# Projections by Strassen's algorithm ahead of the scan, in a Mamba-2 and gated-MLP encoder layer

## The chip, the cores and the metric

One core of a Trainium2 chip runs one encoder layer for two request groups, 1024 prompt tokens and 64 sample tokens, 1088 in all. The measure is the device time of one execution in microseconds (us); lower is better. The core's engines run side by side, each with its own queue in which instructions are taken in order: TensorE (PE in the profile; its loading of weights is listed as PEld), VectorE (DVE), ScalarE (ACT), GpSimd (POOL) and SyncE (SP, which here only starts DMA transfers).

## The reference, cut to what matters

```python
h = rms_norm(x, pre_mix_w)                        # (1088, 1024)
proj = h @ w_in                                   # (1024, 9248): u 1024, v 1024, z 2048, xBC 3072, dt 32, g_a 1024, g_b 1024
u = gelu(u); v = layer_norm(gelu(v))
o_a = u * (blocked 128x128 position mix of v + bias)
xs, B, C = split(silu(causal_conv(xBC, width=4)))
y = ssd_scan(xs, dt, B, C)                        # 4 groups of 8 heads, row tiles of 128 tokens, state carried from tile to tile
o_b = group_rms_norm((y + d_skip * xs) * silu(z))
merged = sigmoid(g_a) * (o_a @ w_branch_a) + sigmoid(g_b) * (o_b @ w_branch_b)
x = x + rms_norm(merged @ w_out)
x = x + rms_norm(relu(rms_norm(x) @ w_up)**2 @ w_down)
```

## The kernel before, in words

Every big product is made three times over. Each operand is held as a rounded part (`hi`, stored as fp32r) and a remainder (`lo`); `split` writes `hi` on ScalarE (line 80) and `lo` on VectorE or GpSimd (line 81), and the product is hi·hi + hi·lo + lo·hi, accumulated in one PSUM bank. There are two forms. `proj_M` (lines 132 to 134) holds 128 tokens still and moves 512 weight columns, 24 matmuls for a row tile and 512 columns. `proj_T` (lines 118 to 120) holds 128 weight columns still and moves 384 or 320 tokens (`TT`), 24 matmuls for each of three token blocks. 1088 tokens are 9 row tiles (`NT`).

The stages follow one another in the program:

1. `first` norms a row tile of the input, `first_T` transposes it into `hT`, and `z_tile` makes z row tile by row tile with `proj_M` (4 x 9 tiles), storing silu pieces in `z_d`; `dt_part` runs among them. The first product needs one row tile only. `v_part` does the same for v (2 x 9 tiles) with gelu and layer norm (STT at line 226, bias at line 227).
2. For each of the 4 groups, `xbc_chunk` makes six 128-column chunks of xBC with `proj_T`, the convolution as one ScalarE pass and three VectorE passes (line 430) for each token block, and transposes to token order. Then the group's scan runs over its 9 row tiles, software-pipelined: `stage_a` (decay matrices: GpSimd line 511, ScalarE line 514, VectorE line 515, and three GpSimd products, lines 519 to 522), one `next(gates)`, which is 24 `proj_T` matmuls of a gate block, then `stage_b` (matmuls `yd`, `yo`, `sn`; VectorE lines 546 to 558, one GpSimd add at line 551) and `stage_c` (four transposes and a store to `ob_d`).
3. `u_chunk` makes u in eight chunks with `proj_T`, and `spatial` mixes positions and multiplies.
4. The branch products: `w_branch_a` on `oa`, then `w_branch_b` in two halves, gate factors applied by `gated` (line 687).
5. `w_out`, then the feed-forward network. Its up product (`UpW`, `up_pass`, lines 966 to 968) and its down product (lines 1116 to 1118) already use the Strassen-Winograd scheme: seven half-size products where eight would be needed, with sums of weight blocks (`UpW.sums`, lines 868 to 875) and of token blocks. The up product moves 272 tokens (`TQ`), the down product moves 512 weight columns.

Tile pools with a fixed number of buffers (`bufs`) set how far a transfer or an engine can run ahead; a scheduler puts each engine's instructions in one fixed order when the kernel is built. Loads go through SP's queue; most stores go through ScalarE's and GpSimd's queues.

## Time and profile before

| | us |
|---|---|
| median of 3 runs | 2266.93 (2264.79 to 2267.3) |
| profiled execution, its own time | 2264.54 |
| span of its trace, first to last instruction | 2262.7 |
| TensorE busy | 2193.6 |
| VectorE busy | 1323.5 |
| ScalarE busy | 924.7 |
| GpSimd busy | 818.9 |

Busy times of different engines overlap. TensorE counts as busy from the start of a matmul to its modelled end, and matmuls overlap in its pipeline, so its pace is read from counts in a stretch, not from the busy share alone.

### The profile page before, as it was taken

To read this page: it belongs to the slowest core of one execution; us is meant where nothing else is said; L and a number is where in the kernel's file an instruction comes from. 1 tells how busy PE (TensorE), PEld (TensorE's weight loads), DVE (VectorE), ACT (ScalarE), POOL (GpSimd) and SP (SyncE) were. 2 spreads that over 40 slices of the span, in tenths; PEclk is the share of its full clock that TensorE was granted. 3 is DMA by queue.
4 is the path that set the end of the run, shared out by engine and by line. 5 is a ranking of instruction groups with operands and counts; after the bars stand their busy time and mean duration, and the time that the engine had idled before them with its cause. 6 is when DMAs were issued, how large, how long until landed. Compare 5 with 4: busy or idle time off the path is not lost.

```text
span 2262.7 us, 33194 instructions
## 1 busy us (share of the span) xinstructions
PE 2193.6 (97%) x12674; PEld 1966.6 (87%) x12674; DVE 1323.5 (58%) x1850; ACT 924.7 (41%) x1788; POOL 818.9 (36%) x798
## 2 busy tenths in 40 slices
PE   8999999999999989999999999998999998999997
PEld 6777778989979979889999999777999997788786
DVE  5322255677677667655722257377555556577777
ACT  5212255445445455433311133255555555433333
...
PEclk9999999999999999999999999999999999999999
...
GB/s 183 70 84 109 58 84 115 58 144 97 80 138 81 105 125 69 129 126 76 97 173 130 134 119 166 135 172 114 147 152 148 140 148 244 163 116 131 172 119 114
DMA packets 315464, 281.07 MB, mean 124 GB/s; under 512 B 40043, under 2 KB 281389, under 8 KB 314793
## 3 DMA queue, kind: packets, MB, share of 16 engines
q1 hardware_dynamic: 283336, 240.71, 35.8%
...
q8 instruction: 100, 1.64, 0.3%
q14 instruction: 60, 0.48, 0.1%
HBM read 203.96 MB, written 74.93 MB: 123 GB/s over the span
## 4 chain that ended last, share of the span: by engine, by line
PE 67%; issue 12%; POOL 8%; DVE 5%; DMA 4%; ACT 3%; SPq 0%; ACTq 0%; POOLq 0%; DVEq 0%
PE ps L119 8%; PE ps L118 8%; PE ps L120 8%; PE X L968 3%; PE X L966 3%; PE X L967 3%; PE X L1117 3%; PE X L1118 3%; PE X L1116 3%; PE ps L1117 2%; PE ps L1116 2%; PE ps L1118 2%; DMA raw<-w_branch_b 2%; PE ps L706 2%; PE ps L705 2%
## 5 line engine op out<-in xcount | busy, mean ns | idle before, releaser
L118 PE MATMUL ps<-hTh,wh 128*128 128x384 f32 (+1 forms) x1152 | 384.4, 334 | 5.5 <-ACT raw L419 5.5
L120 PE MATMUL ps<-hTh,wl 128*128 128x384 f32 (+1 forms) x1152 | 386.4, 335 | 0.0
L119 PE MATMUL ps<-hTl,wh 128*128 128x384 f32 (+1 forms) x1152 | 384.5, 334 | 0.0
L81 POOL TENSOR_TENSOR wl<-raw,wh 128x1024 fp32r<-128x1024 f32 x74 | 182.4, 2467 | 270.3 <-ACT wh L80 268.0
L80 ACT ACTIVATE wh<-raw 128x1024 fp32r<-128x1024 f32 x128 | 135.3, 1057 | 268.9 <-PE ps L119 98.2
L118 PEld LDWEIGHTS ps<-hTh,wh 128*128 128x128 f32 x1152 | 217.1, 188 | 11.6 <-ACT raw L419 6.0
L120 PEld LDWEIGHTS ps<-hTh,wl 128*128 128x128 f32 x1152 | 216.9, 188 | 9.8 <-issue 9.7
L119 PEld LDWEIGHTS ps<-hTl,wh 128*128 128x128 f32 x1152 | 217.2, 189 | 7.9 <-issue 7.3
L132 PE MATMUL ps<-wh,hTh 128*128 128x512 f32 (+1 forms) x432 | 171.3, 398 | 1.0 <-ACT hTh L177 0.9
L133 PE MATMUL ps<-wl,hTh 128*128 128x512 f32 (+1 forms) x432 | 170.4, 396 | 0.9 <-DVE wl L81 0.9
L134 PE MATMUL ps<-wh,hTl 128*128 128x512 f32 (+1 forms) x432 | 171.0, 396 | 0.2 <-DVE hTl L178 0.2
L430 DVE SCALAR_TENSOR_TENSOR acc<-raw,cw,acc 128x384 f32<-128x384 f32 (+1 forms) x216 | 134.6, 626 | 33.6 <-ACT acc L428 27.7
L966 PE MATMUL X<-hb,wu 128*128 128x272 f32 x512 | 147.7, 291 | 1.9 <-ACT ev L973 1.0
L967 PE MATMUL X<-hb,wu 128*128 128x272 f32 x512 | 147.6, 289 | 0.3 <-DVE hb L790 0.3
L968 PE MATMUL X<-hb,wu 128*128 128x272 f32 x512 | 146.1, 290 | 0.0
L514 ACT ACTIVATE bc<-bc,pcum 128x128 f32<-128x128 f32 (+1 forms) x288 | 90.8, 384 | 89.3 <-POOL bc L511 88.4
L1110 POOL TENSOR_TENSOR wd<-wd,wd 128x1024 f32<-128x1024 f32 x32 | 85.8, 2684 | 113.6 <-DVE dl L81 74.5
L705 PE MATMUL ps<-ob,wh 128*128 128x384 f32 (+1 forms) x384 | 125.4, 327 | 0.0
L706 PE MATMUL ps<-ob,wl 128*128 128x384 f32 (+1 forms) x384 | 125.4, 327 | 0.0
L704 PE MATMUL ps<-ob,wh 128*128 128x384 f32 (+1 forms) x384 | 125.4, 326 | 0.0
L80 ACT ACTIVATE dh<-wd 128x1024 fp32r<-128x1024 f32 x56 | 59.1, 1055 | 153.2 <-PE ps L1117 91.9
L81 DVE TENSOR_TENSOR dl<-xd,dh 128x1024 fp32r<-128x1024 f32 x56 | 100.4, 1818 | 1.8 <-PE X L968 1.2
...
## 6 DMA issues: line engine op xcount, KB each, us to landing
...
xd<-rc_d SPq DMA_DIRECT2D x112, 256.0 KB, 3.9
...
wd<-w_down SPq DMA_DIRECT2D x16, 1024.0 KB, 6.0
...
```

Source lines behind the costliest of these rows:

```text
L80: s.activation(hi, src, AF.Copy)
L81: (lo_eng or v).tensor_tensor(out=lo, in0=src, in1=hi, op=ALU.subtract)
L118: pe.matmul(ps[:, :n], wh[:, k, :], hh[:, k, :n], start=(k == 0), stop=False)
L119: pe.matmul(ps[:, :n], wh[:, k, :], hl[:, k, :n], start=False, stop=False)
L120: pe.matmul(ps[:, :n], wl[:, k, :], hh[:, k, :n], start=False, stop=(k == 7))
L132: pe.matmul(ps[:R, :], hh[:, k, o:o + R], wh[:, kk, :], start=(k == 0), stop=False)
L134: pe.matmul(ps[:R, :], hl[:, k, o:o + R], wh[:, kk, :], start=False, stop=(k == 7))
L705: pe.matmul(ps[:, :n], wh[:, k, :], ob[:, 4 + kk, :], start=False, stop=False)
L706: pe.matmul(ps[:, :n], wl[:, k, :], ob[:, kk, :], start=False, stop=(k == 7))
L966: pe.matmul(ps, wh[:, k, :], bh[:, k, :], start=start and k == 0, stop=False, skip_group_check=chain)
L967: pe.matmul(ps, wh[:, k, :], bl[:, k, :], start=False, stop=False, skip_group_check=chain)
L968: pe.matmul(ps, wl[:, k, :], bh[:, k, :], start=False, stop=k == 3, skip_group_check=chain)
```

## The change

All products of the normed input move into one first stage and use the Strassen-Winograd scheme.

- The normed rows are written once into seven block combinations, each as hi and lo and for two token halves (`hb`, 28 tiles of 4 x 272). Rows 0 to 3 give two of them at once; `second(m)` norms row 4 + m, makes the differences and the other five by transposes (`put`).
- z and v: three passes of 1024 columns (`plan`), each seven products of 4 row blocks x 12 matmuls with 512 moving columns. The weight sums are built by GpSimd from pieces loaded again for each product (`build`). The 64 sample tokens get 8 matmuls in each of four products (`sample`).
- u, xBC and the gates: 24 pairs of chunks (256 columns), each two token halves (`t_pass`) of seven products x 12 matmuls with 272 moving tokens. What used to follow a chunk follows in steps between the products of the next pass (`todo`): gelu and the layer norm of v (`ln_row`) for u, the convolution over 1091 columns at a time for xBC (`x_conv`), tanh for the gates; dt and the spatial mix run among the gate passes (`side`). Results go to DRAM: u, the gates, xs, B and C, the layer-normed v, the dt tables and the branch-A input.
- The scan then runs alone over all 36 (group, row tile) pairs in one pipeline with a load step (`stage_0`) one tile ahead. Between two tiles comes one block of the branch products (`fill`: 24 blocks of branch A, then 24 of the first half of branch B), merged through `mg_d` in DRAM. The add at line 551 moves from GpSimd to VectorE.
- All DMA transfers of these stages go through SP's queue. The second half of branch B, `w_out` and the feed-forward network stay, with other buffers out of the same pools.

```diff
-    ws0 += list(ws)
-    ws = ws0
-    first(2)
-    first_T(1)
-    for i in range(NT):
-        z_tile(ws, 0, i)
...
-    for gi in range(1, G):
...
-        for i in range(NT):
-            z_tile(ws, gi, i)
-            next(dtg, None)
...
-gates = gate_gen()
-for _ in range(3):
-    next(gates)
...
-                next(gates)
...
-                g.tensor_tensor(out=y[:R], in0=y[:R], in1=xi[:R], op=ALU.add)
...
+    def sums(self, k):
+        x, tt = self.src, self.eng.tensor_tensor
+        if k == 0:
+            x["s1"], x["s2"] = (t.rearrange("p (k n) -> p k n", k=4) for t in self.t12)
+            tt(out=x["s1"], in0=x["a21"], in1=x["a22"], op=ALU.add)
+            tt(out=x["s2"], in0=x["s1"], in1=x["a11"], op=ALU.subtract)
+        elif k == 1:
+            x["s3"] = x["a21"]
+            y = (x["a21"], x["a11"]) if self.flip else (x["a11"], x["a21"])
+            tt(out=x["s3"], in0=y[0], in1=y[1], op=ALU.subtract)
+        else:
+            x["s4"] = x["a12"]
+            tt(out=x["s4"], in0=x["a12"], in1=x["s2"], op=ALU.subtract)
...
+def t_pass(w, wn, tt, hbt, evs, ev, xp, todo):
...
+    def prod(j, ps, start=True, chain=True):
+        wh, wl = w.w[j]
+        bh, bl = hbt(TB[j], tt)
+        for k in range(4):
+            pe.matmul(ps, wh[:, k, :], bh[:, k, :], start=start and k == 0, stop=False, skip_group_check=chain)
+            pe.matmul(ps, wh[:, k, :], bl[:, k, :], start=False, stop=False, skip_group_check=chain)
+            pe.matmul(ps, wl[:, k, :], bh[:, k, :], start=False, stop=k == 3, skip_group_check=chain)
...
+    if first:
+        wn.sums(0)
+    step(0)
+    prod(1, Z, chain=False)
+    ev[0](Z, s0)
...
+hb = [[[hbp.tile([P, 4, TQ], F32R, tag="hb", bufs=28, name="hb") for x in "hl"] for tt in range(2)] for n in range(7)]
...
+    def k4(name):
+        return pm.tile([P, 1024], F32, tag="k4", bufs=6, name=name)
...
+    def second(m):
+        row_norm(4 + m)
+        xa, xb = rows[m], rows[4 + m]
+        b12, b22 = xb[:, 0:512], xb[:, 512:1024]
+        e1, e4 = xa[:, 0:512], xa[:, 512:1024]
+        e3 = s2("e3")
+        v.tensor_tensor(out=e1, in0=b12, in1=e1, op=ALU.subtract)
+        v.tensor_tensor(out=e3, in0=b12, in1=b22, op=ALU.subtract)
+        v.tensor_tensor(out=b12, in0=b22, in1=e1, op=ALU.subtract)
+        put(b12, 4, m)
+        put(e3, 5, m)
+        put(e1, 3, m)
+        v.tensor_tensor(out=e4, in0=e4, in1=b12, op=ALU.subtract)
+        put(e4, 6, m)
+        put(b22, 2, m)
...
+    plan = [(pr, n) for pr in range(3) for n in ("P2", "P1", "P6", "P5", "P7", "P3", "P4")]
...
+        elif n == "P6":
+            t = kept[pr, q] = w_piece(pr, 1, 1, q, "v2", True)
+            u = w_piece(pr, 0, 0, q, "w11", False)
+            tt_(out=t, in0=t, in1=u, op=ALU.subtract)
+            u = w_piece(pr, 0, 1, q, "w12", False)
+            tt_(out=t, in0=t, in1=u, op=ALU.add)
...
+    def raw(j):
+        return wpool.tile([P, 1024], F32, tag="raw", bufs=2, name="wr")
...
+    cols = [OFF_U + p * 256 for p in range(4)] + [OFF_X + p * 256 for p in range(12)] + [OFF_GA + p * 256 for p in range(8)]
...
+    def passes(k, ev, after=None, more=None):
+        nonlocal todo
+        for tt in range(2):
+            fs, post = ev(tt)
+            t_pass(W[k], W.get(k + 1), tt, hbt, evs, fs, xp, todo)
+            todo = post
+            if more:
+                more()
+        new_w(k + 2)
...
+    def c_layout(c, dst, p, tt):
+        for h in range(2):
+            d = dst[2 * p:2 * p + 2].rearrange("j p c -> p j c")
+            nc.sync.dma_start(out=d[:, :, h * 512 + tt * 256:h * 512 + tt * 256 + 256], in_=c[:, 2 * h:2 * h + 2, 0:256])
+            nc.sync.dma_start(out=d[:, :, 1024 + h * 32 + tt * 16:1024 + h * 32 + tt * 16 + 16], in_=c[:, 2 * h:2 * h + 2, 256:TQ])
...
+        def ln_row(i):
+            R = ROWS[i]
+            vt = pu.tile([P, D], F32, tag="vt", bufs=2, name="vt")
+            nc.sync.dma_start(out=vt[:R], in_=v_d[i * P:i * P + R, :])
...
+            v.scalar_tensor_tensor(out=vt[:R], in0=vt[:R], scalar=r[:R], in1=lnw[:R], op0=ALU.mult, op1=ALU.mult)
+            g.tensor_tensor(out=vt[:R], in0=vt[:R], in1=lnb[:R], op=ALU.add)
+            nc.sync.dma_start(out=vn_d[i * P:i * P + R, :], in_=vt[:R])
...
+                def p0():
+                    q[0] = pu.tile([P, 4 * TQ], F32, tag="q", bufs=1, name="q")
+                    s.activation(q[0], C, AF.Square)
+                def p1():
+                    g.tensor_scalar(out=q[0], in0=q[0], scalar1=GC * GA3, scalar2=GC, op0=ALU.mult, op1=ALU.add)
+                def p2():
+                    v.tensor_tensor(out=q[0], in0=C, in1=q[0], op=ALU.mult)
+                def p3():
+                    s.activation(q[0], q[0], AF.Tanh)
+                def p4():
+                    v.scalar_tensor_tensor(out=C, in0=q[0], scalar=1.0, in1=C, op0=ALU.add, op1=ALU.mult)
...
+            def tap(k):
+                v.scalar_tensor_tensor(out=t[0][:, :L], in0=r[:, k:k + L], scalar=cw[:, k * 24 + c:k * 24 + c + 1],
+                                       in1=t[0][:, :L], op0=ALU.mult, op1=ALU.add)
...
+            def p5():
+                v.scalar_tensor_tensor(out=t[0][:, :L], in0=r[:, :L], scalar=1.0, in1=t[0][:, :L], op0=ALU.add, op1=ALU.mult)
...
+        def side():
+            with tc.tile_pool(name="pdt", bufs=1, side="right") as wk:
+                yield from dt_part(wk)
+            yield
+            with tc.tile_pool(name="psp", bufs=1, side="right") as wk:
+                for c in range(8):
+                    yield from spatial(c, wk)
...
+    def fill_a(ts):
+        for c in range(8):
+            w = wT(a["w_branch_a"][0], c * P, lo_eng=(v, g)[c % 2])
+            for t in ts:
+                o, n = TT[t]
+                gtt = gate_in(sp, c, t)
+                gated(gtt, proj_T(w, oa, t), gtt[:, :n], n)
+                nc.sync.dma_start(out=mg_d[c][:, o:o + n], in_=gtt[:, :n])
+                yield
...
+    def fill_b(ts):
...
+                gtt = gate_in(sp, 8 + c, t)
+                mgt = sp.tile([P, 384], F32, tag="mgt", bufs=2, name="mgt")
+                nc.sync.dma_start(out=mgt[:, :n], in_=mg_d[c][:, o:o + n])
+                gated(gtt, proj_b(w, 0, t), gtt[:, :n], n)
+                v.tensor_tensor(out=gtt[:, :n], in0=mgt[:, :n], in1=gtt[:, :n], op=ALU.add)
+                nc.sync.dma_start(out=mg_d[c][:, o:o + n], in_=gtt[:, :n])
+                yield
...
+    def fill():
+        for t in range(3):
+            load_oa(t)
+        yield from fill_a((0, 1))
+        for t in range(2):
+            load_ob(0, t, bslot(t, "ob0"))
+        yield from fill_a((2,))
+        for t in range(2):
+            load_ob(1, t, bslot(t, "ob1"))
+        yield from fill_b((0, 1))
+        for gi in range(2):
+            load_ob(gi, 2, bslot(2, f"ob{gi}"))
+        yield from fill_b((2,))
...
+    def stage_0(gi, i):
...
+        d["BT"], d["CT"], d["btok"] = (sp.tile([P, P], F32, tag=n, bufs=3, name=n) for n in ("BT", "CT", "btok"))
+        nc.sync.dma_start(out=d["BT"][:, :R], in_=bc_d[gi][:, tok:tok + R])
+        nc.sync.dma_start(out=d["CT"][:, :R], in_=bc_d[4 + gi][:, tok:tok + R])
...
+            bc = sp.tile([P, 4, P], F32, tag="bc", bufs=6, name="bc")
+            nc.sync.dma_start(out=bc[:R, :, :R], in_=ac_d[h0:h0 + 4, i, 0:R].partition_broadcast(R))
...
+        d["xs"] = sp.tile([P, 512], F32, tag="xs", bufs=3, name="xs")
+        nc.sync.dma_start(out=d["xs"][:R], in_=xs_d[tok:tok + R, gi * 512:(gi + 1) * 512])
+        nc.sync.dma_start(out=d["btok"][:R], in_=btok_d[tok:tok + R, gi * P:(gi + 1) * P])
+        d["sz"] = sp.tile([P, 512], F32, tag="sz", bufs=3, name="sz")
+        nc.sync.dma_start(out=d["sz"][:R], in_=z_d[tok:tok + R, gi * 512:(gi + 1) * 512])
...
+            v.tensor_tensor(out=y[:R], in0=y[:R], in1=xi[:R], op=ALU.add)
...
+    tiles = [(gi, i) for gi in range(G) for i in order]
+    NR = len(tiles)
+    S = None
+    for k in range(NR + 3):
+        if k < NR:
+            stage_0(*tiles[k])
+        if 1 <= k <= NR:
+            stage_a(*tiles[k - 1])
+        if k >= 1:
+            next(filler, None)
+        if 2 <= k <= NR + 1:
+            gi, i = tiles[k - 2]
+            S = stage_b(gi, i, S)
+            if i in (7, 8):
+                state_out(gi, i, S)
+        if k >= 3:
+            stage_c(*tiles[k - 3])
+    for _ in filler:
         pass
```

## Rows read from the trace of the kernel before

**Rows 1.** The page's first part, and its granted-clock line over 40 slices:
```profile
PE 2193.6 (97%) x12674; PEld 1966.6 (87%) x12674; DVE 1323.5 (58%) x1850; ACT 924.7 (41%) x1788; POOL 818.9 (36%) x798
...
PEclk9999999999999999999999999999999999999999
```

**Rows 2.** Busy time by stage (stretch, its length, engines' busy us with counts, clock, DMA):
```profile
0.00:336.60 336.60, 326.30 (x1462) 253.88 (x1463) 126.80 (x163) 107.26 (x160) 68.86 (x109) 1.00 0.31 99
336.60:1002.00 665.40, 640.21 (x3915) 587.02 (x3914) 461.42 (x687) 326.93 (x809) 338.89 (x397) 0.99 0.37 104
1002.00:1137.00 135.00, 135.00 (x855) 133.43 (x855) 80.66 (x155) 45.83 (x87) 38.94 (x36) 1.00 0.32 92
1137.00:1421.50 284.50, 284.50 (x1730) 284.50 (x1729) 115.36 (x123) 66.59 (x72) 119.10 (x62) 1.00 0.48 147
1421.50:2262.70 841.20, 807.61 (x4720) 707.77 (x4719) 539.28 (x724) 378.05 (x661) 253.10 (x195) 0.98 0.47 148
```

**Rows 3.** The same view inside four stretches of one kind of product:
```profile
150.00:250.00 100.00, 100.00 (x432) 78.28 (x431) 23.13 (x27) 20.95 (x29) 10.53 (x18) 1.00 0.30 101
1150.00:1300.00 150.00, 150.00 (x912) 150.00 (x911) 31.98 (x47) 20.99 (x19) 50.57 (x29) 1.00 0.45 139
1600.00:1850.00 250.00, 250.00 (x1989) 250.00 (x1988) 140.42 (x248) 136.40 (x272) 61.67 (x48) 1.00 0.48 147
2000.00:2200.00 200.00, 200.00 (x867) 160.31 (x866) 147.42 (x148) 69.53 (x79) 58.26 (x26) 1.00 0.45 138
```

**Rows 4.** TensorE in order of time at the start (start, length, instruction, count):
```profile
11.16 0.79 PE L132 MATMUL ps<-wh,hTh 128*128 128x512 f32 x1 [0.91 <-ACT hTh L177]
...
15.90 1.03 PE L174 MATMUL tp<-ident,xn 128*128 128x128 f32 x8
```

**Rows 5.** One GpSimd group, each shape apart (busy us, mean ns):
```profile
L227 POOL TENSOR_TENSOR vst<-vst,lnb 128x1024 f32<-128x1024 f32 x8 | 19.3, 2410 | 3.7 <-DVE vst L226 3.7
```

**Rows 6.** VectorE groups of the kind that the passes hold, same view:
```profile
L884 DVE TENSOR_TENSOR wu<-wr,wu 128x512 fp32r<-128x512 f32 x80 | 55.7, 699 | 17.6 <-ACT wu L880 17.5
...
L979 DVE TENSOR_TENSOR C<-Z,ev 128x272 f32<-128x272 f32 x32 | 14.1, 442 | 19.9 <-PE Z L968 15.0 <-ACT C L1034 2.7 <-ACT C L1025 0.7
...
L226 DVE SCALAR_TENSOR_TENSOR vst<-vst,rs,lnw 128x1024 f32<-128x1024 f32 x8 | 10.2, 1279 | 0.7 <-POOL rs L142 0.6
```

**Rows 7.** Busy time in the last scan and two other stretches, as rows 2:
```profile
948.00:1002.00 54.00, 51.10 (x305) 43.91 (x304) 38.79 (x47) 23.39 (x63) 38.50 (x43) 1.00 0.51 141
2050.00:2100.00 50.00, 50.00 (x218) 40.20 (x217) 40.32 (x39) 14.87 (x16) 21.86 (x9) 1.00 0.42 126
1850.00:1900.00 50.00, 50.00 (x389) 49.49 (x388) 25.14 (x46) 25.70 (x49) 4.68 (x3) 1.00 0.76 243
```

**Rows 8.** VectorE groups of the scan, view as rows 5:
```profile
L515 DVE TENSOR_TENSOR bc<-bc,cb 128x512 f32<-128x512 f32 x64 | 42.7, 679 | 14.7 <-POOL xs L522 6.1 <-PE cb L503 4.8 <-ACT bc L514 3.5
...
L558 DVE SCALAR_TENSOR_TENSOR y<-y,rs,snw 128x512 f32<-128x512 f32 x32 | 35.8, 1117 | 20.9 <-POOL rs L142 20.6
...
L546 DVE TENSOR_TENSOR S<-S,elast 128x512 f32<-128x512 f32 x32 | 32.9, 1027 | 0.6
L554 DVE TENSOR_TENSOR y<-y,sz 128x512 f32<-128x512 f32 x32 | 32.4, 1012 | 28.0 <-POOL y L551 27.9
...
L548 DVE TENSOR_TENSOR S<-tp,S 128x512 f32<-128x512 f32 x32 | 21.8, 682 | 1.2 <-PE tp L540 1.2
```

**Rows 9.** VectorE groups that go with the branch products, view as rows 5:
```profile
L81 DVE TENSOR_TENSOR wl<-raw,wh 128x1024 fp32r<-128x1024 f32 x54 | 71.7, 1332 | 43.4 <-ACT wh L80 43.3
...
L687 DVE SCALAR_TENSOR_TENSOR gtt<-gtt,ps 128x384 f32<-128x384 f32 x32 | 17.6, 549 | 42.5 <-PE ps L706 37.8 <-DMA gtt<-gates_d 4.3
...
L81 DVE TENSOR_TENSOR ob<-st,ob 128x1536 fp32r<-128x1536 f32 x8 | 14.0, 1771 | 9.6 <-ACT ob L80 9.5
```

**Rows 10.** One VectorE line of the scan (durations min/median/max):
```profile
L546 DVE TENSOR_TENSOR S<-S,elast x32: 675/1055/1574, 444.1 to 988.7; 128x512 f32<-128x512 f32 x32
```

**Rows 11.** DMA issues (KB each, median us to landing), from 1850 to 1900 us:
```profile
wd<-w_down SPq DMA_DIRECT2D x4, 1024.0 KB, 10.1
```

1247 lines of the change are left out of this document (764 added, 483 removed).

## The prediction

> **What bounds the kernel now.** First the engines' busy shares and the granted clock [rows 1]: TensorE is busy 97% of the span and its granted clock is 0.9 or more of the upper level (2.4 GHz) in every slice, so time is saved by giving TensorE less to stream, as long as no other engine takes over. VectorE is next with 58%, but that is a mean over unlike stages. So the second view is the busy time by stage [rows 2]: the normed input's z and v (0 to 336.6), xBC, scans and most gates (to 1002.0), the last gates and u (to 1137.0), the branch products (to 1421.5), then `w_out` and the feed-forward network (841.2 us). The change touches the first 1421.5 us. VectorE is busy 0.38, 0.69, 0.60 and 0.41 of the four stages, GpSimd 0.51 of the second.
>
> The third view gives TensorE's pace, since busy time cannot [rows 3]: 100 us / 432 = 0.2315 us for a matmul with 512 moving columns, 150 / 912 = 0.1645 with 384 and 320, 250 / 1989 = 0.1257 with 272 (the up product), 200 / 867 = 0.2307 with 512 in the down product. The reader should see that the pace does not fall in proportion: 272 columns are 0.75 of the mean 363, but cost 0.764. That is a small fixed part, and the two Strassen products run at it without a gap.
>
> **z and v.** Before: 54 tiles x 24 = 1296 matmuls x 0.2315 = 300.0, 72 transposes at 1.03 / 8 = 0.129 [rows 4] = 9.3, dt 72 x 0.1645 = 11.8; the remaining 336.6 - 321.1 = 15.5 is the start (the first matmul is at 11.16 [rows 4]) and small waits. After: three passes of 7 x 4 x 12 + 4 x 8 = 368 matmuls, 1104 x 0.2307 = 254.7, and 112 + 8 transposes = 15.5. The start is not shown. From below it is the old 15.5. From above: six buffers hold the norm weight and rows 0 to 3 and 8, so row 5 is loaded only when `second(0)` is through, and the first product P6 waits for the rows; four times a norm (1.28), four differences (1.03 each) and five evictions (0.68 each) (all priced as in the parts below) are 35 us of VectorE against 22 us of P2 and P1, so some 13 more, 29. I take 18, near the lower end, because P5 can go between. Sum 288.2, a gain of 48.4. The weight sums are GpSimd's: ten 1024-wide operations a pass at 2.4 [rows 5] are 24 of 85 us, hidden; without that cover they would be 72.
>
> **u, xBC and gates.** Before, 48 chunks x 72 x 0.1645 = 568.5; after, 24 pairs x 168 x 0.1257 = 506.8, a gain of 61.7. dt moves here: 120 x 0.1257 = 15.1. The transposes to token order and the spatial mix stay: some 220 + 144 instructions at 0.129 = 47. So 569 us of TensorE. What can hold it back is VectorE, in whose queue the evictions that free PSUM stand behind the convolution. A u pass has TensorE at 84 x 0.1257 = 10.56; VectorE has 3.5 splits at 0.70, three evictions at 0.44, two 1088-wide operations at 1.28 x 1088/1024 = 1.36 [rows 6], and 9/8 of a layer-norm row (about 2.56): 9.4. An xBC pass has TensorE at 11.7 with nine transposes; VectorE has four 1091-wide operations (5.5), 2.45 of splits and 1.9 of evictions, 9.8, which is 0.84. Between nothing and the full excess of a slot with eviction, tap and split over one product (some 1 us) I take 0.5 for an xBC pass, 12 in 24, and 0.6 for a u pass, 5 in 8. Gate passes have half of that load: nothing. Three joints between pools: 11. Sum 596.5. The loads for pair k + 2 are asked for after pair k and land within a pass.
>
> **From there to the scan:** tables and first tiles must be loaded and the branch-A input split before TensorE has work: between 5 and 20, taken as 12.
>
> **The scan.** In the last scan before, 305 matmuls ran in 54 us for seven tiles [rows 7]. 7 x 26 are the scan's, the other 123 are gate blocks and cost 123 x 0.1645 = 20.2; (51.1 - 20.2) / 7 = 4.4 us of TensorE for a tile. With a filler block of 24 x 0.1645 = 3.95 a tile needs 8.35. About 40 of the 48 blocks fall into the scan: 36 x 4.4 + 40 x 3.95 = 316 of TensorE. VectorE, from its own rows: two at 0.68, the decay product 1.03, three with a PSUM operand at 0.68, 1.01 and 1.12 [rows 8], and the moved add, priced as the decay product at 1.03 (both operands in SBUF): 7.59. For 36 tiles, less 4 x 2.74 where a group starts with no state, 262. State copies 12 x 0.68 = 8; 40 `gated` at 0.55 = 22; 16 merges at about the same = 9; half of 24 weight splits at 1.33 = 16; ten splits of branch inputs at 1.77 = 18 [rows 9]. Together 335: VectorE, not TensorE, bounds this stage, with 9.3 us a tile where TensorE wants 8.35. From below the stage takes TensorE's 316 (if the contention inside these means goes with GpSimd's add); from above, VectorE reached 40.32 of 50 at most, 0.81, in any stretch I looked at [rows 7], so 335 / 0.81 = 414. I take 0.92, as VectorE was never the bound in those stretches: 364.
>
> **After it:** 8 blocks left, 31.6; the second half of branch B 24 x 3.95 = 94.8; joint 6. Sum 132.4. The rest, 841.2 us [rows 2], changes only in which buffers it takes: nothing, give or take 5.
>
> **The sum:** 288.2 + 596.5 + 12 + 364 + 132.4 = 1393 against 1421.5, so 28.4 less: a span of 2234.3. The profiled execution took 1.8 more than its span, and the median of the runs is 2.4 above that execution: 2238, say 2237, 1.3% faster.
>
> **The rivals.**
> *TensorE keeps the scan (0.15).* If VectorE stays off the path, the scan takes 316, 48 less: 2189. For it: the contended means of [rows 8] (line 546 takes 0.675 to 1.574 [rows 10]) would shrink when GpSimd loses an add. Against: GpSimd gets weight splits in return.
> *VectorE holds the scan at its old share (0.22, the other side).* One mechanism, one place: VectorE's fixed order in the scan, where the chain of one tile (square on ScalarE, root on GpSimd, line 558) leaves holes: 20.6 us of its idle time were waits for that root [rows 8]. At 0.81 the stage takes 414, 50 more than my sum: 2287. It decides from 364 + 28 = 392 us, 10.9 us a tile.
> *VectorE and GpSimd take turns (0.10).* Line 546 has both operands in SBUF and takes 0.675 at best and 1.574 at worst [rows 10], while line 548, with one operand in PSUM, has a mean of 0.682 [rows 8]: such operations wait for GpSimd's. If they exclude each other fully, the u passes are hit: VectorE's two-operand work is 3.5 x 0.70 + 2 x 1.36 + 1.44 = 6.6, GpSimd's two sums (2.4), one 1088-wide operation (up to 2.56) and 9/8 of 2.41 [rows 5] are 7.7; 14.3 against 10.56 is 30 in 8 passes, 25 more than in my sum: 2262, next to no gain. Against: the means that I add up hold these waits already. The Trainium skill (SBUF — State Buffer, section "SBUF: two separate sides") says the same as a rule: a VectorE instruction with two SBUF inputs and a GpSimd one that reads SBUF lock each other out of a shared port pair for a whole instruction. By that rule the u stage would be the loss, and the spread of line 546 agrees with it.
> *Late loads (0.05).* Everything goes through one queue, and the scan moves 36 tiles (51 MB), 24 weight chunks (13), gates and merged blocks (17) and branch inputs (8): 89 MB in 364 us, 244 GB/s. The stretch with 243 GB/s had the DMA engines busy 0.76 [rows 7] and 1 MB loads landing after 10.1 us [rows 11]; `stage_0` asks one tile, about 10 us, ahead. Two us late for each tile would be 72: 2309.
> *The narrow matmuls give nothing back (0.03).* At 568.5 / 4032 = 0.141 a matmul the passes cost what the chunks did: 2299. Against: 1989 at 0.1257 without a gap [rows 3].
>
> **How the numbers follow.** My own case (0.45) is 2237, by its own terms 2215 to 2262. With the two rivals around it, TensorE's scan below and VectorE's above, the range is 2185 to 2290; the late loads and the narrow matmuls stay outside. A measurement of this kernel tells some 0.2% (4.5 us) from no change. Slower takes the three rivals above 2271 less a little (0.27); no change gets part of the turn-taking and the upper end of my case (0.07); faster the rest, 0.66.
>
> **What would show it.** Right: a first `t_pass` near 290 us; up to the scan near 900; passes at 10.6 us for gates and 12.1 for xBC; output stores of the scan about 10 us apart, with VectorE busy over 0.9 there and TensorE some 0.85; the stage behind the branches still 841. Wrong: a scan with VectorE at 0.8 and tiles 11 us apart, or waits of TensorE in the xBC passes for evictions by VectorE, or loads of the scan that land after their tile's turn. My weakest number is VectorE's share in the scan: 0.01 of it is 4 us.

## The result and the profile after

The changed kernel takes 2370.49 us (median of four runs, 2366.20 to 2383.30) against 2265.86 (2264.19 to 2267.30): a ratio of 1.0471 [1.0429, 1.0514], 105 us slower. The forecast was 2237, with a range up to 2290; the time lies outside it on the side that had 0.27. The profiled execution took 2383.3 us, with a span of 2381.5, the longest of the four; a second profile of the same kernel (c0_after) has a span of 2369.2.

The page's first part and its granted-clock line over 40 slices, to be read against [rows 1]:

```profile
PE 2153.5 (90%) x13154; PEld 1926.8 (81%) x13154; DVE 1610.6 (68%) x2086; ACT 1039.9 (44%) x1985; POOL 929.5 (39%) x812
...
PEclk8899999899999999799999989999999999999999
```

TensorE is busy 40 us less than before, as the change meant, but in a span 119 us longer: its share falls from 97 to 90%. VectorE gains 287 us of work. The granted clock falls under 0.9 of the upper level in five slices, which it did in none before. Busy time by stage, as [rows 2], with the boundaries at the first `t_pass` matmul, the last one, the scan's first product, its last store to `ob_d` and the last branch product; then two stretches of the first stage:

```profile
0.00:330.20 330.20, 285.50 (x1225) 225.91 (x1226) 208.51 (x233) 139.47 (x235) 119.10 (x89) 0.95 0.54 164
330.20:983.00 652.80, 587.97 (x4510) 575.22 (x4509) 459.36 (x640) 303.66 (x600) 233.69 (x236) 0.96 0.42 126
983.00:996.00 13.00, 1.36 (x8) 0.84 (x6) 0.00 (x0) 1.35 (x3) 2.34 (x1) 0.61 0.83 222
996.00:1382.70 386.70, 343.46 (x1946) 292.75 (x1946) 319.50 (x404) 170.18 (x432) 252.16 (x264) 0.94 0.85 243
1382.70:1533.30 150.60, 125.69 (x757) 122.80 (x756) 87.09 (x87) 48.14 (x56) 68.08 (x28) 0.93 0.71 215
1533.30:2381.50 848.20, 809.47 (x4717) 709.30 (x4716) 536.14 (x724) 377.10 (x661) 254.09 (x195) 0.98 0.46 147
0.00:100.00 100.00, 57.54 (x245) 43.82 (x246) 64.01 (x75) 42.13 (x92) 44.58 (x49) 0.86 0.43 135
200.00:330.20 130.20, 130.03 (x562) 103.89 (x561) 82.81 (x97) 56.53 (x84) 43.31 (x28) 1.00 0.50 151
```

| stage | forecast | after | too short by | c0_after |
|---|---|---|---|---|
| z and v | 288.2 | 330.2 | 42 | 328.8 |
| passes of u, xBC, gates | 596.5 | 652.8 | 56 | 648.2 |
| to the scan | 12 | 13.0 | 1 | 12.9 |
| scan, first product to last store | 364 | 386.7 | 23 | 382.7 |
| rest of the branches | 132.4 | 150.6 | 18 | 149.3 |
| `w_out` and feed-forward | 841.2 | 848.2 | 7 | 847.3 |

Every term erred to the same side. Three places show how.

**The start.** The first 100 us hold 245 TensorE instructions, 435 before. About 120 are transposes: 120 x 0.129 + 125 x 0.2307 = 44 us of work, 56 lost where I had put 18. The timeline of SP's queue, rows of the input alone (`row_load`, line 321):

```profile
3.43 1.03 SPq L321 DMA_DIRECT2D row<-x_prompt  x2
4.50 0.57 SPq L321 DMA_DIRECT2D row<-x_sample  x1
...
39.41 0.34 SPq L321 DMA_DIRECT2D row<-x_prompt  x1
...
53.10 1.22 SPq L321 DMA_DIRECT2D row<-x_prompt  x2
...
67.58 0.33 SPq L321 DMA_DIRECT2D row<-x_prompt  x1
```

Row 4 is asked for at 39.4, when the sample row has left its buffer, rows 5 and 6 at 53, row 7 at 68: each `second(m)` waits for its row, and P6, the first product that needs these rows, for all four.

**The joint between u and xBC.** The timeline of ScalarE, GpSimd and VectorE, three instructions of the last layer-norm row, the first write to xBC's tile `R`, and the eviction of the first product of three passes (line 239, one in each pass; the expectations below call it the second):

```profile
428.13 0.38 ACT L239 ACTIVATE ev<-X 128x272 f32<-128x272 f32 x1
438.69 0.40 ACT L239 ACTIVATE ev<-X 128x272 f32<-128x272 f32 x1 [0.47 <-DVE C L629]
...
468.19 1.21 DVE L663 TENSOR_REDUCE mu<-vt 64x1 f32<-64x1024 f32 x1 [2.92 <-DMA vt<-v_d]
...
473.01 1.28 DVE L670 SCALAR_TENSOR_TENSOR vt<-vt,rs,lnw 64x1024 f32<-64x1024 f32 x1 [3.61 <-POOL rs L129]
...
474.36 2.33 POOL L671 TENSOR_TENSOR vt<-vt,lnb 64x1024 f32<-64x1024 f32 x1 [1.39 <-DVE vt L670]
...
481.25 0.42 DVE L738 TENSOR_TENSOR R<-Z,ev 128x256 f32<-128x256 f32 x1 [6.96 <-DMA new_gmlp_v_sample<-vt]
...
481.79 0.40 ACT L239 ACTIVATE ev<-X 128x272 f32<-128x272 f32 x1 [9.72 <-DVE R L739]
```

The first xBC pass has its product by 438.7, but may write `R` only at 481.25, when the store of the last layer-norm row has left the memory that `R` takes over. TensorE stands still; the next such step comes 43.1 us on, in place of 12.

**The operations of the passes.** Groups of VectorE and GpSimd in the xBC passes (490 to 755 us), mean ns of one; priced in the forecast at 1360, 700 and 2400 / 2 [rows 5, 6]:

```profile
L772 DVE SCALAR_TENSOR_TENSOR acc<-R,cw,acc 128x1091 f32<-128x1091 f32 x65 | 112.7, 1753 | 13.1 <-ACT acc L769 12.8
L204 DVE TENSOR_TENSOR wu<-wr,wu 128x512 fp32r<-128x512 f32 x53 | 45.3, 862 | 18.4 <-ACT wu L200 17.6 <-PE tp L794 0.6
...
L192 POOL TENSOR_TENSOR wr<-wr 128x512 f32<-128x512 f32 x11 | 23.4, 2128 | 0.0
```

### The profile page after: what moved, and what is told of

The parts are those of the page before. It is cut to its first block, busy times and chain, and to the rows that moved or that the text cites. A ratio compares the mean times of both kernels' runs of the same rounds, so it can differ in the third digit from the quotient of the medians.

```text
span 2381.5 us, 35955 instructions
## 1 busy us (share of the span) xinstructions
PE 2153.5 (90%) x13154; PEld 1926.8 (81%) x13154; DVE 1610.6 (68%) x2086; ACT 1039.9 (44%) x1985; POOL 929.5 (39%) x812
## 4 chain that ended last, share of the span: by engine, by line
PE 42%; DMA 12%; DVE 12%; issue 5%; ACT 4%; POOL 3%; SPq 1%; ACTq 0%; DVEq 0%; POOLq 0%
PE X L1487 3%; PE X L1489 3%; PE X L1488 3%; DVE acc L772 3%; PE X L1638 2%; PE X L1639 2%; PE X L1637 2%; DMA wr<-w_in 2%; PE ps L1638 2%; PE ps L1639 2%; PE ps L1637 2%; DMA xs<-xs_d 2%; DVE wu L204 2%; DMA mg_d<-gtt 1%; PE Y L1487 1%
## 5 line engine op out<-in xcount | busy, mean ns | idle before, releaser
L226 PE MATMUL X<-hb,wu 128*128 128x272 f32 x768 | 228.9, 299 | 26.4 <-ACT ev L252 9.4
L227 PE MATMUL X<-hb,wu 128*128 128x272 f32 x768 | 224.6, 293 | 0.0
L228 PE MATMUL X<-hb,wu 128*128 128x272 f32 x768 | 224.1, 294 | 0.0
L79 POOL TENSOR_TENSOR wl<-raw,wh 128x1024 fp32r<-128x1024 f32 x52 | 129.0, 2485 | 167.5 <-ACT wh L78 121.9
L226 PEld LDWEIGHTS X<-hb,wu 128*128 128x128 f32 x768 | 147.8, 193 | 32.1 <-ACT ev L252 11.5
L1041 PE MATMUL ps<-ob,wh 128*128 128x384 f32 (+1 forms) x384 | 131.2, 343 | 24.4 <-DMA st<-ob_d 18.7
L1487 PE MATMUL X<-hb,wu 128*128 128x272 f32 x512 | 148.3, 291 | 4.1 <-ACT ev L1510 2.3
L227 PEld LDWEIGHTS X<-hb,wu 128*128 128x128 f32 x768 | 148.3, 193 | 0.1
L1488 PE MATMUL X<-hb,wu 128*128 128x272 f32 x512 | 148.0, 290 | 0.0
L1489 PE MATMUL X<-hb,wu 128*128 128x272 f32 x512 | 146.7, 291 | 0.9 <-DVE wu L1405 0.9
L228 PEld LDWEIGHTS X<-hb,wu 128*128 128x128 f32 x768 | 147.4, 193 | 0.0
L204 DVE TENSOR_TENSOR wu<-wr,wu 128x512 fp32r<-128x512 f32 x120 | 103.3, 867 | 51.4 <-ACT wu L200 50.6
L772 DVE SCALAR_TENSOR_TENSOR acc<-R,cw,acc 128x1091 f32<-128x1091 f32 x72 | 124.2, 1742 | 16.0 <-ACT acc L769 15.8
L1631 POOL TENSOR_TENSOR wd<-wd,wd 128x1024 f32<-128x1024 f32 x32 | 85.7, 2681 | 116.5 <-DVE dl L79 77.8
L1042 PE MATMUL ps<-ob,wh 128*128 128x384 f32 (+1 forms) x384 | 129.6, 338 | 0.5 <-DVE ob L79 0.5
L78 ACT ACTIVATE wh<-raw 128x1024 fp32r<-128x1024 f32 x72 | 75.8, 1055 | 103.2 <-DMA raw<-w_branch_b 61.1
L226 PE MATMUL Y<-hb,wu 128*128 128x272 f32 x384 | 113.3, 295 | 7.8 <-ACT wu L200 6.1
L227 PE MATMUL Y<-hb,wu 128*128 128x272 f32 x384 | 112.3, 293 | 0.0
L228 PE MATMUL Y<-hb,wu 128*128 128x272 f32 x384 | 112.0, 293 | 0.0
```

Of the source, the lines that this page charges most:

```text
L78: s.activation(hi, src, AF.Copy)
L204: v.tensor_tensor(out=l, in0=self.src[TN[j]], in1=h, op=ALU.subtract)
L226: pe.matmul(ps, wh[:, k, :], bh[:, k, :], start=start and k == 0, stop=False, skip_group_check=chain)
L227: pe.matmul(ps, wh[:, k, :], bl[:, k, :], start=False, stop=False, skip_group_check=chain)
L228: pe.matmul(ps, wl[:, k, :], bh[:, k, :], start=False, stop=k == 3, skip_group_check=chain)
L772: v.scalar_tensor_tensor(out=t[0][:, :L], in0=r[:, k:k + L], scalar=cw[:, k * 24 + c:k * 24 + c + 1], in1=t[0][:, :L], op0=ALU.mult, op1=A ...
```

## The experiments

The theories, as the expectations number them. **1:** one queue; a store that waits for its producer holds up the loads behind it. **2:** VectorE's own work, with its waits for the root on GpSimd, sets the scan. **3:** late releases of tiles (rows at the start, one pool after another at the joints). **Lock:** VectorE's operations with both operands in SBUF wait while GpSimd's run. **4:** the scan's loads come late. **5:** the traffic of the blocks slows the scan. **6:** no engine alone.

All runs, with the end of the first stage, the length of the passes, and the mean step between the scan's 36 stores to `ob_d`. Kernels that leave a stage alone end the first at 326.5 to 333.9, take 648 to 653 for the passes and 10.4 to 10.7 for a tile; the four totals of the changed kernel span 17 us. What is smaller is not read.

| run | us | z, v end | passes | tile |
|---|---|---|---|---|
| c0_after | 2371.0 | 328.8 | 648.2 | 10.36 |
| e1_store_q | 2382.8 | 325.9 | 661.1 | 10.57 |
| e2_ln_late | 2407.8 | 328.0 | 682.3 | 10.73 |
| e8_row8 | 2365.8 | 321.0 | 650.1 | 10.45 |
| e13_start | 2368.9 | 316.2 | 652.9 | 10.49 |
| e6_nosums | 2333.9 | 327.8 | 606.4 | 10.54 |
| e12_sums_v | 2359.1 | 328.8 | 629.4 | 10.50 |
| e14_ln2 | 2382.6 | 328.3 | 659.3 | 10.47 |
| e7_ob_early | 2351.2 | 328.9 | 650.7 | 10.43 |
| e3_scan_alone | 2385.4 | 330.1 | 649.9 | 9.98 |
| e4_deep | 2368.6 | 328.3 | 650.2 | 10.33 |
| e10_bare | 2257.0 | 329.6 | 653.1 | 8.10 |
| e11_root | 2375.8 | 326.5 | 651.1 | 10.50 |
| e15_relief | 2390.3 | 333.9 | 650.4 | 10.42 |
| e16_norm_act | 2359.4 | 329.6 | 648.5 | 10.09 |
| e17_traffic | 2377.4 | 327.5 | 651.4 | 10.59 |
| c2_all (median of 4) | 2358.2 | 316.9 | 639.9 | 10.51 |
| c4_parts (median of 5) | 2320.7 | 314.9 | 628.1 | 10.36 |

### The kernel again, and the queue

> The changed kernel as it is, for a second profile beside the first one. Every theory expects the same stage times as in the first: products of z and v 330 us, the passes of u, xBC and the gates 653, from there to the start of the second half of branch B 406, then 144, then 848; a few us less in all, since the first profile is of the slowest of four runs (2383 against 2366 to 2373). What differs between the two by more than that is spread, and no experiment is read finer than it.

```diff
...
-nc.sync.dma_start(out=mg_d[c][:, o:o + n], in_=gtt[:, :n])
+nc.scalar.dma_start(out=mg_d[c][:, o:o + n], in_=gtt[:, :n])
...
```

> Every store of the new stages (z, v, u, layer-normed v, xs, B, C, dt tables, gates, branch-A input, merged blocks, scan outputs and states) goes through ScalarE's queue in place of SP's, as most did before the change; loads stay with SP. Theory 1 (one queue: a store that waits for its producer holds up the loads behind it, which is where the late weights and the late loads of the scan come from): TensorE's idle time falls in the u passes, at the joint between u and xBC and in the scan, tiles of the scan go from 10.5 to about 9.3 us, and the whole gains 60 us or more. Theory 2 (VectorE's own chain in the scan, through the root on GpSimd, sets the pace there) and theory 3 (late releases of tiles, at the start and where one pool follows another): within 15 us of the changed kernel, with the hole at the joint and the 56 us lost in the first 100 still there.

It gained nothing: the passes took 13 us more and the tile did not move. The eight u passes (eight steps between evictions of first products) went from 100.7 to 110.6. Theory 1 falls, as far as a store's place in SP's queue goes.

### The start

```diff
-rows[i] = k4("row")
+rows[i] = k4("row") if i < 8 else wpool.tile([P, 1024], F32, tag="raw", bufs=2, name="row")
```

> At the start the sample row (row 8) is put into one of the two buffers for raw weight pieces, so that one of the six row buffers is free and row 4 is loaded at once, not after the sample row has been transposed at 39 us. Theory 3 (buffers: each second(m) waits for a row that could not be loaded yet): the first second() comes about 10 us earlier and the stage of z and v ends at about 315 to 322 in place of 330. Theory 2 applied to the start (VectorE and GpSimd in each other's way, row norms and weight splits): no earlier end, within 4 us of 330.

and in e13_start also

```diff
-split(src[k, q], hi, lo, g if k < 3 else v)
+split(src[k, q], hi, lo, v)
```

> Beside row 8 in a raw buffer (8 us gained in the first stage), the remainders of the first three products' weights are made by VectorE and not by GpSimd, whose 2.5 us each fall together with row norms and differences that took 2.3 to 5.7 us where others of the same shape took 0.7 to 1.3. Lock theory at the start: those fall to 0.7 to 1.3, and the first stage ends 8 to 15 us earlier than with the buffer alone, near 308. Buffers alone: no further gain, within 4 us of 321.

321.0 and 316.2. The buffer gave 8 us, as theory 3 said. The remainders gave 5 more, between what the lock (8 to 15) and buffers alone (less than 4) asked for; that is less than the spread of this stage, but the two later kernels that hold both edits end it at 316.9 and 314.9. TensorE has done 247 instructions by 100 us in c0_after, 280 in e8_row8 and 298 in e13_start. Together the two edits are 13 of the 42 us. In e13_start rows 5 and 6 are still asked for at 41 us and row 7 at 56, so most of the start is still there, in buffers and in the chain of row norms; it wasn't tried further. The totals of these two runs don't show the gain, which is of the size of their spread.

### The layer-norm rows

In e2_ln_late `ln_row` goes from the last step of a u pass into `side()`, ahead of dt:

```diff
 def side():
+    with tc.tile_pool(name="pln", bufs=1, side="right") as pln:
...
+        for i in range(NT):
+            ln_row(i)
+            if i % 3 == 2:
+                yield
```

> The layer norm of v, nine rows, moves from the u passes to the first gate passes, three rows at a time ahead of the dt part. Theory 3 (the first xBC pass writes into memory that the last layer-norm row holds, and waits for its store): the hole of 34 us at the joint goes, u passes fall from 12.6 us to about 11, and the gate passes take some 5 to 8 us more; 35 to 45 us less in all. Theory 1 (the queue alone holds the u passes and the joint): the weights of the next pair stay late, and less than 15 us are gained.

The eight u passes fell from 100.7 to 85.7 us (10.7 a pass; the forecast has 10.56 of TensorE), the step at the joint from 43.2 to 18.9: 39 us gained there, as theory 3 said. But the gate passes took 73 more. Who TensorE waited for in them:

```profile
PE ps L845 <- ACT wdh L78: 58.4, 1, 58.4
```

dt's first product stands in TensorE's queue behind few passes, and its operand is made in a pool that opens when the last row is through. The hole moved with the rows.

```diff
-if lnq:
-    ln_row(lnq.pop(0))
-if len(lnq) == 1:
-    ln_row(lnq.pop(0))
+for _ in range(2):
+    if lnq:
+        ln_row(lnq.pop(0))
```

> The nine layer-norm rows of v go two to a pass into the first u passes, in place of one to a pass with the last two behind the last u pass. Same work on every engine, an earlier place. Theory 3 (the hole at the joint is the chain of the last rows up to their store, which holds the memory that the first xBC pass writes): the step from the last u pass's to the first xBC pass's second eviction falls from 43 us to 20 or less, the u passes take up to 10 us more together, and 10 to 25 us are gained. If the memory of the pool is not what is waited for, the joint stays over 35 us.

The joint fell to 21.2, as expected, but the u passes rose from 100.7 to 133.0: 11 us lost in the passes. So no place that was tried is free of the price. A row is a chain over four queues (load, sum on VectorE, mean on GpSimd, two passes on ScalarE, root on GpSimd, VectorE, GpSimd, store), and what stands behind a link in its queue waits with it; that this chain is the price was read from the waits, not shown by a run that shortens it. Nine rows cost 39 us where they are, and more in both other places.

### The weight sums and the lock

In e6_nosums `TPair.sums` does nothing and the products use plain blocks; in e12_sums_v it runs on VectorE:

```diff
-W[k] = TPair(w_in, cols[k], raw, factor, t12, g if k else v, True)
+W[k] = TPair(w_in, cols[k], raw, factor, t12, v, True)
```

> The passes of u, xBC and the gates leave out GpSimd's four weight sums for each pair of chunks (the products use plain blocks instead of the sums, so u, xBC and the gates are other numbers; everything else is as before). Lock theory (VectorE's operations with both operands in SBUF wait while GpSimd's run): the convolution's tap falls from a mean of 1.74 us towards its shortest, 1.36, the remainders of the weight splits from 0.87 to about 0.70, and a pass of xBC from 11.9 to about 11.2, 20 to 30 us in all. Rival (the means are long because of DMA traffic or the tap's own shape): taps stay at 1.7 us, and the passes gain less than 8 us.

The same groups in the same stretch, without the sums:

```profile
L762 DVE SCALAR_TENSOR_TENSOR acc<-R,cw,acc 128x1091 f32<-128x1091 f32 x67 | 89.9, 1351 | 11.3 <-ACT acc L759 10.9 <-POOL cst L757 0.3
L194 DVE TENSOR_TENSOR wu<-wr,wu 128x512 fp32r<-128x512 f32 x83 | 56.2, 687 | 21.0 <-ACT wu L190 17.4 <-PE tp L784 3.0
```

The tap falls from 1753 to 1351 ns, the remainder from 862 to 687, and the passes by 42 us. Nothing else in the tap changed: it had waited for GpSimd. In the changed kernel the 27 of its 65 taps that have no GpSimd operation beside them take 1347 ns in the mean, the 38 others 2041. One that starts while a sum runs ends 1.16 us after it (timelines of GpSimd and VectorE, the changed kernel):

```profile
502.07 1.76 POOL L195 TENSOR_TENSOR wr<-wr,t 128x512 f32<-128x512 f32 x1
503.01 1.98 DVE L772 SCALAR_TENSOR_TENSOR acc<-R,cw,acc 128x1091 f32<-128x1091 f32 x1
...
506.12 1.34 DVE L772 SCALAR_TENSOR_TENSOR acc<-R,cw,acc 128x1091 f32<-128x1091 f32 x1
```

The Trainium skill (SBUF — State Buffer, section "SBUF: two separate sides") states this as an exclusive lock on a shared port pair between a VectorE operation with two SBUF inputs and a GpSimd operation that reads SBUF; the trace agrees, with 1351 against 1753 ns.

> The weight sums of the passes are made by VectorE in place of GpSimd: four operations of 0.69 us for a pair, 1.4 for a pass, but no taps at 1.74 us beside GpSimd's sums. Leaving the sums out gained 42 us in the passes. If the lock alone was that price, VectorE's 1.4 us more for a pass and 1.2 less for three taps nearly cancel in the xBC passes, and the u and gate passes, where VectorE has room, gain 15 to 25 us together. If the price was the sums' lateness (the weight splits wait for them), about the same. If VectorE's total is the limit in the xBC passes whatever its operations wait for, they go from 11.9 to 12.5 or more and the whole gains nothing.

The passes gained 19 us, in other places than I wrote: xBC 8.5 (265.4 for 273.9), the u passes with the joint 9.4, the gates nothing. The taps were at 1348 ns here too. So 19 of the 42 us come back when the sums only leave GpSimd, and 23 are what they still cost on VectorE. Whether the 19 are the lock or the sums' lateness wasn't separated: the expectation has the same time for both.

### The hole ahead of the second half

What TensorE waited for there in the changed kernel (1382 to 1440 us):

```profile
PE ps L1041 <- DMA st<-ob_d: 18.7, 1, 18.7
```

```diff
 for gi in range(2):
     load_ob(gi, 2, bslot(2, f"ob{gi}"))
+for t in range(2):
+    for gi in (2, 3):
+        load_ob(gi, t, bslot(t, f"ob{gi}"))
 yield from fill_b((2,))
```

> The inputs of the second half of branch B (groups 2 and 3, first two token blocks) are loaded and split into the buffers that groups 0 and 1 leave, before the last eight blocks of the first half, and not into a pool that is opened only when the scan's pool is closed; the merged result takes that pool's tiles instead. Theory 3 (a joint between pools): the hole between the two halves (19 us of TensorE waiting for the split, 19 for the load before it) goes, and 15 to 25 us are gained. If the hole is the last blocks waiting for their weights (one 512 KB chunk for each narrow block), less than 8 us are gained.

From the end of the passes to the last branch product it took 530.8 us in place of 544.9, and the whole 20 less. Theory 3 holds here.

### The scan

In e3_scan_alone `next(filler, None)` leaves the loop over tiles.

> The branch blocks no longer go between the tiles of the scan; all 48 come after it. Tiles of the changed kernel end 10.4 us apart (363 us for 35 steps), and VectorE has 7.6 us of work for a tile without a block. Theory 2 (VectorE's work and its waits for the root on GpSimd set the pace): with the block's 1.7 us gone the tiles come 8 to 9 us apart, the scan takes about 300, the blocks behind it 190 to 210, and the whole is 80 to 110 us longer. Theory 4 (each tile's own loads, asked for one tile ahead, come late; the block is filler that costs nothing): tiles stay near 10 us apart, and the whole is 170 to 200 us longer. If the blocks and their own traffic (weights, gates, merged blocks) are what makes the tile late, tiles fall to 7 us or less and the whole is at most 40 us longer.

This told nothing of what it was meant to: the scheduler put the blocks among the tiles again (branch A's matmuls run from 1030 to 1267 us, the scan to 1361).

> The scan's loads are asked for two tiles ahead in place of one (one more buffer each for B, C, xs, silu(z) and two for the decay rows). Theory 4 (late loads: GpSimd waited 39 us for decay rows and 18 us for xs in the scan): tiles fall from 10.4 to 9.5 us or less, the scan gains 30 us. Theory 2 (VectorE and its root): tiles stay within 0.2 of 10.4, the whole within 8 us of the changed kernel (2366 to 2373).

The tile stayed (10.33). But only some of the late loads were taken away. What GpSimd waited for from 1000 to 1360 us, in c0_after and then in e4_deep, the decay rows (`bc`) and xs:

```profile
POOL bc L1141 <- DMA bc<-ac_d: 40.2, 30, 3.5
POOL xdt L1148 <- DMA xs<-xs_d: 16.5, 11, 3.0
```

```profile
POOL bc L1141 <- DMA bc<-ac_d: 59.6, 33, 7.1
POOL xdt L1148 <- DMA xs<-xs_d: 1.4, 1, 1.4
```

So theory 4 falls for xs; for the decay rows, for which GpSimd waited longer still, it wasn't tested. The kernel before waited 41.9 us for them too, in its four scans.

> Branch A and the first half of branch B are left out (no blocks, no weights, no gates and no merged blocks beside the scan; the merged result is the second half of branch B alone). What is left between the passes and the second half is the scan with its own loads. Theory 2 (VectorE's and GpSimd's work with their waits sets the pace): tiles fall from 10.4 us to 8 to 8.5, since VectorE loses 1.7 us of work a tile and GpSimd 0.8; the tile of the kernel before took 8.2. Theory 5 (the traffic of the blocks beside the tile's own, DMA engines 0.85 busy, makes the tile late): tiles fall to 7.5 or less. If they stay at 9.5 or more, the tile's own chain from its loads is the limit and the blocks cost nothing.

A tile without a block takes 8.10 us. With 40 blocks for 36 tiles, 4.4 us of TensorE a tile cost 2.3 us of stage: the filler hides half of itself. Part of that may be the clock, which wasn't separated: TensorE was granted 0.77 in the bare scan and 0.95 with the blocks. VectorE's share in the bare scan (1020 to 1290 us) is 219.61 / 270 = 0.81, without any block:

```profile
1020.00:1290.00 270.00, 196.38 (x893) 134.77 (x891) 219.61 (x295) 116.18 (x351) 183.33 (x224) 0.77 0.65 179
```

> The product with the root (the last VectorE step of a tile) is written one step of the pipeline later, beside the transposes of its tile, so that VectorE need not wait for the square on ScalarE and the root on GpSimd. VectorE waited 46 us for that root in the scan. Theory 2 in this form (the root's chain makes the holes in VectorE): most of the 46 us go, tiles 9.5 us or less, 25 us or more gained. Rival (the holes only move to the next wait, since GpSimd and the loads are as late as before): within 10 us of the changed kernel, with VectorE's idle time under other names.

Nothing gained: VectorE still waited 45 us for the root. Only its place in the program was changed, and its place in VectorE's queue hardly moved.

In e16_norm_act and e15_relief the root and the norm weight go to ScalarE, ahead of and behind the transposes in `stage_c`; in e15_relief the add goes to TensorE as well (the last two lines):

```diff
-v.scalar_tensor_tensor(out=y[:R], in0=y[:R], scalar=r[:R], in1=snws[gi][:R], op0=ALU.mult, op1=ALU.mult)
+s.activation(y[:R], y[:R], AF.Identity, scale=r[:R])
...
-s.activation(ob[:, :, :R], tp[:, :, :R], AF.Copy)
+for q in range(4):
+    s.activation(ob[:, q, :R], tp[:, q, :R], AF.Identity, scale=snT[:, gi * 4 + q:gi * 4 + q + 1])
...
-v.tensor_tensor(out=y[:R], in0=y[:R], in1=xi[:R], op=ALU.add)
+pe.matmul(yd[:R], ident[:R, :R], xi[:R], start=False, stop=True, skip_group_check=True)
```

> In the scan VectorE loses two operations of each tile (1.3 and 0.96 us): the add of D times xs is made by TensorE as one more product into yd's bank, the root is applied by ScalarE before the transposes and the norm weight by ScalarE when they are evicted, four operations for one. Loads, blocks and GpSimd's work stay. Theory 2 (VectorE's work at the share of 0.8 that it reaches beside GpSimd sets the tile): 2.3 / 0.8 = 2.8 us less a tile, as far as TensorE lets it (8.4 us with the blocks, 9.2 with the added product), so tiles of about 9.2 to 9.5 us in place of 10.4 and 30 to 40 us gained. Theory 5 (traffic: DMA engines 0.85 busy, GpSimd waits for decay rows and xs) or the root's latency: tiles stay over 10 us, less than 12 us gained.

> Of the relief only the half that costs TensorE nothing: the root and the norm weight are applied by ScalarE (one product before the transposes, four evictions for one after), the add of D times xs stays with VectorE. VectorE loses 1.3 us of work a tile and its waits for the root, GpSimd, TensorE and the traffic stay. Theory 2 (VectorE's work sets the tile): 1.3 / 0.8 = 1.6 us less, tiles of 8.8 to 9.2 us in place of 10.4, 40 us gained or more. Theory 6 (no engine alone: TensorE's own work with a block is 8.7 us a tile, and the remaining 1.6 come from its waiting for transposes and states in a fixed order): tiles stay over 10 us, less than 12 us gained. Theory 5 (traffic): the same as theory 6.

> The blocks beside the scan load no gates and no merged block and branch A's blocks store none: two fixed tiles stand in for them (so the merged result is another; weights, matmuls, gate products, merges and the second stores stay). Some 18 of the scan's 95 MB go, and with them the chain from a store of a merged block to its load. Theory 5 (traffic, DMA engines 0.85 busy): loads of the scan's own land sooner, GpSimd's waits for decay rows and xs (39 and 18 us) halve, tiles fall to 9.6 us or less, 25 us or more gained. Theories 2 and 6: within 10 us of the changed kernel, tiles at 10.2 to 10.5.

Busy time from 1020 to 1370 us, in this order: the changed kernel again (c0_after), e15_relief, e16_norm_act, e17_traffic:

```profile
1020.00:1370.00 350.00, 315.81 (x1808) 269.77 (x1807) 292.73 (x372) 152.09 (x389) 229.81 (x239) 0.95 0.83 243
```

```profile
1020.00:1370.00 350.00, 323.32 (x1787) 263.15 (x1786) 216.34 (x297) 188.15 (x516) 215.33 (x238) 0.97 0.82 237
```

```profile
1020.00:1370.00 350.00, 323.65 (x1892) 280.97 (x1891) 260.63 (x344) 194.22 (x529) 223.78 (x240) 0.96 0.85 249
```

```profile
1020.00:1370.00 350.00, 313.76 (x1748) 266.49 (x1749) 288.66 (x362) 147.94 (x384) 225.76 (x236) 0.93 0.71 197
```

With some 16 MB less to move in this stretch (197 against 243 GB/s) the tile stays at 10.59: theory 5 falls, as far as the blocks' traffic goes. With VectorE's share down from 0.84 to 0.62 and TensorE's product in its place it stays at 10.42 (e15_relief makes another y; the work on each engine is as described). With VectorE at 0.745 and TensorE's matmuls unchanged it falls to 10.09, 12 us in all, where theory 2 asked for 40; and c4_parts below, which holds the same edit, is at 10.36 again, so even these 12 us are not shown. Both runs give ScalarE some 40 us more work in this stretch (152 to 188 and 194), so what VectorE's relief alone would give is not shown either. What is shown is that taking a tenth (e16_norm_act) or a quarter (e15_relief) of VectorE's work out of this stretch does not bring the time that theory 2 promised. TensorE is busy 0.90 of the time, 0.925 when VectorE is relieved, at a granted clock of 0.93 to 0.97, where the last scan of the kernel before had 1.00 [rows 7]. Theory 6 is nearest, by what is left; that TensorE and its clock, or the late decay rows, are the limit was not shown by a run of its own.

### The parts together

> All parts that gained or should gain together: inputs of the second half early (18 us), row 8 in a raw buffer and the first remainders on VectorE (12 in the first stage), weight sums of the passes on VectorE (12 to 19), layer-norm rows early (10 to 25), VectorE relieved in the scan (30 to 40). If the prices are separate and add up, 2370 - 82 to 114 gives 2256 to 2288, about the kernel before (2266). If a part only moves its wait to the next joint, it ends above 2300.

c2_all holds two parts that gained nothing by themselves (e14_ln2, e15_relief), and with e15_relief's added product it makes another y as well. It takes 2358.23 us, 1.0413 [1.0381, 1.0444] of the kernel before, above the 2300 that were to mean a wait that only moves. c4_parts holds e7_ob_early, e13_start, e12_sums_v and e16_norm_act:

> The parts that gained by themselves, together: inputs of the second half early (18 us in its single run), row 8 in a raw buffer with the first remainders on VectorE (12 in the first stage), weight sums of the passes on VectorE (12 to 19), root and norm weight on ScalarE in the scan (12). If the prices are separate they add up to 54 to 61: 2309 to 2317, still some 45 to 50 above the kernel before, which is what the layer-norm rows (39, at the joint and in the u passes), the rest of the start and the scan would then be. If the waits share a cause, it ends above 2330.

2320.70 us (2316.78 to 2329.51), a little more than the 2309 to 2317 expected, a ratio of 1.0252 [1.0225, 1.0279]. Its stages, to set beside c0_after's 328.8, 648.2, 544.9 and 847.3:

```profile
0.00:314.90 314.90, 281.73 (x1224) 223.54 (x1225) 204.00 (x239) 139.32 (x235) 103.32 (x83) 0.97 0.56 172
314.90:943.00 628.10, 578.40 (x4509) 568.28 (x4508) 441.94 (x732) 303.63 (x600) 89.28 (x144) 0.97 0.43 131
943.00:1469.10 526.10, 467.04 (x2710) 412.26 (x2710) 366.15 (x458) 260.55 (x635) 314.10 (x292) 0.94 0.83 244
1469.10:2317.80 848.70, 810.20 (x4716) 711.33 (x4714) 538.15 (x722) 377.32 (x661) 254.81 (x195) 0.98 0.46 146
```

14 + 20 + 19 us: the start and the sums add up fully. The 19 are the hole's: from the scan's last store to the last branch product it takes 131.6 us in place of 149.3, while the scan's 36 stores span 362.5 against 362.7, so its relief gave nothing here. Half of the loss of 105 us is accounted for by three separate causes that could be taken away. No version that does all of the work beats the kernel before.

## Why the prediction was wrong, point by point

- **Paces: right.** 562 instructions in 130.2 us are 0.2317, the forecast's 0.2307 [rows 3]; a u pass without the rows took 10.7 us (e2_ln_late) against 10.56 of products, so the narrow matmuls do give back what [rows 3] promised. That rival falls. An xBC pass took (759.9 - 481.8) / 23 = 12.1 us, as forecast, but with some luck: its taps were priced at 1360 ns and took 1753, and the 0.5 us added for VectorE covered that. Without the sums a pass took 11.4.
- **The start: mis-sized**, 18 with an upper bound of 29; about 56 in the first 100 us. I named the mechanism (six buffers, late rows) and then priced it by VectorE's work alone. Each `second` also waits for a load that is asked for late (8 us by e8_row8) and, it seems, for VectorE held up by GpSimd (5 more in e13_start); the other 29 of the 42 us stay open.
- **"9/8 of a layer-norm row (about 2.56)": the step that failed in the u passes.** It counted a row as VectorE's busy time. The u passes took 12.6 us in place of 11.2, and the three joints far more than 11: 43.1 less a pass of 12 is 31 at the one between u and xBC. Without the rows both shrink, by 39 us together (e2_ln_late).
- **"The weight sums are hidden": failed.** I asked if GpSimd had the time, and it had. Leaving them out of the passes gained 42 us; 19 of them came back when the sums went to VectorE, where the taps no longer wait. The rival of turn-taking had this mechanism and placed it in the u passes alone, at 25; its "against" (the means hold these waits already) fell: [rows 6] are means beside another GpSimd.
- **The gates** were given no stall in the forecast; the 16 passes took 223 us against 16 x 10.56 + 15.1 + 18.6 = 203.
- **To the scan: right**, 12 against 13.0.
- **The scan: two parts near, one wrong.** VectorE's sum was 335, measured 319.5; 40 blocks, measured (1946 - 36 x 26 - 48) / 24 = 40. Its share was 0.92 in the forecast and 319.5 / 386.7 = 0.826 in the trace, next to the old 0.81, which was the rival with 0.22. But that rival's mechanism, holes for the root, is not shown: removing operation and wait gained a quarter of what it asks for in e16_norm_act and nothing in c4_parts. The step that failed is the share, and with it "VectorE, not TensorE, bounds this stage": VectorE was to be busy 0.92 as the bound, reached 0.826, and cutting its work did not reliably shorten the tile. Late xs loads and the blocks' traffic fell as causes (e4_deep, e17_traffic), late decay rows did not. What sets the tile at 10.1 to 10.4 stays open between them, TensorE's own work, its lower clock and the order of the queues.
- **The rest of the branches:** the joint that I put at 6 was a hole of 18.7 us; loading ahead of it took 14 to 20 us away.
- **The feed-forward network:** 7 us more, a little past the bound of 5. No run was made for it.
- **A term that was missing: TensorE's clock.** The forecast's paces come from rows with a granted clock of 1.00 [rows 3, 7]. The mean over the whole execution was 0.959 here and 0.992 before: (1 - 0.959) x 2381.5 = 98 us of full pace not granted against 18, so at most 80 us more, and less than that, as TensorE stood still in part of the time. An estimate from the two traces, half of the step behind each matmul that began at the lower level (steps over 0.48 us counted as 0.48), is 58 us against 11, with 20 of them in the scan. It lies inside the shortfalls above and doesn't come on top of them; no run changed the clock alone.
- **The range** took one rival at a time beside an otherwise right sum. But five terms had left out a wait or its size, all on the same side: 42 + 56 + 23 + 18 + 7 = 146 of the 147 us between 2234.3 and 2381.5.
